# Four 16-row copies from SBUF to SBUF between the first loads of the GpSimd queue, in an eight-expert MoE kernel

## The chip, the core and the metric

The kernel runs on one core of a Trainium2 chip. The metric is the device time of one execution in microseconds (us); the median of 4 runs before the change is 183.47 us (183.39 to 183.78).

## The reference

Eight experts each apply a two-layer network to their own 256 rows of x. E = 8, T = 256, H = 512, M = 2048, all in float32:

```python
h = np.matmul(x, w1) + b1[:, np.newaxis, :]
h = np.maximum(h, 0)
return (np.matmul(h, w2) + b2[:, np.newaxis, :]).astype(np.float32)
```

x is (8, 256, 512), w1 is (8, 512, 2048), w2 is (8, 2048, 512); b1 and b2 are (8, 2048) and (8, 512). Each expert's w1 and w2 are 4 MB each in HBM, so the weights alone are 67 MB.

## The kernel before, in words

**Types and tiles.** The products run in fp16. DMAs issued by GpSimd convert on the way: they read float32 from HBM and write fp16 to SBUF. A w1 or w2 tile is 128 x 8192 fp16 (2 MB in SBUF, three buffers of each kind); an x tile is 128 x 1024 fp16 (256 KB, four buffers). The x of experts 0 and 1 comes as float32 by the SyncE and ScalarE queues (L188) and is cast by VectorE (L201). An output tile is 128 x 1024 float32, 512 KB, three buffers.

**Work per expert.** `first_product` (L108) multiplies the transposed x by w1 in 16 groups of four matmuls; ScalarE adds b1 and applies the ReLU to each (L120). Half-way, TensorE transposes the x of the next expert (L100). `second_product` (L151) starts from b2 by a one-row matmul (L163) and adds 32 matmuls of 512 columns (L175); VectorE and ScalarE each copy one half to the output tile (L138, L139). Step s of the last loop (L243) does the first product of expert s and the second of expert s - 3 (LAG = 3).

**What sets the order of the loads.** Nearly all transfers are DMAs issued by GpSimd, in one order written out by hand: the list `ring` (L221 to L241). Each entry has a step at which it may go, a function and its arguments; `ordered` keeps program order. The list begins at s = 1 with w1[1], and has for each later s the x of expert s (`load_x`, L69), the w1 of expert s (`load_w1`, L75), the w2 of expert s - 3 (`load_w2`, L85), and from s = 6 the store of the output of expert s - 6 (`flush`, L132). After it come eight pieces of the last expert's w2 (`load_w2_piece`, L91) with stores between them. w1[0] and the b2 row (L191, 8 KB) are issued ahead of the list. The last expert's output goes by SyncE and ScalarE (L142, L143, L149).

**What a DMA on GpSimd waits for.** A load waits until its buffer is free: a w1 tile for the first product of the expert three back, a w2 tile for the second product of the expert three back. Besides, the built program has eight completion semaphores for GpSimd's DMAs, given out in turn. A DMA that gets a semaphore again waits until the DMA that had it before, eight places ahead in GpSimd's order, has landed. GpSimd issues in order, so whatever stands behind a waiting DMA waits with it. In the text, w1[3] is the w1 of expert 3, out[0] the store of expert 0's output.

Of the kernel before, what the change touches and what calls it, by code (L numbers as in the profile page):

```python
# [11 lines left out]
def kernel(  # L12
# [9 lines left out]
    nc = tc.nc  # L22
    fp32 = mybir.dt.float32
# [3 lines left out]
    P = 128  # L27
# [4 lines left out]
    LAG = 3  # L32
# [5 lines left out]
    def ordered(ins):  # L38
        return tc.keep_in_program_order(ins)

    singles = ctx.enter_context(tc.tile_pool(name="singles", bufs=1))
# [14 lines left out]
    b2_sb = singles.tile([1, E * H], fp16)  # L56
    b1_rows = singles.tile([E * 2, M // 2], fp32)
    b1T = singles.tile([P, nJ, E], fp32)

    x16 = [None] * E  # L60
    xT = [None] * E
# [68 lines left out]
    def flush(e):  # L130
        dst, src = pending.pop(e)
        ordered(nc.gpsimd.dma_start(out=dst, in_=src))  # L132

    def store(e, po, c0, c1, split):
        w = c1 - c0
        pool = out_pool if w == H else singles
        out_sb = pool.tile([P, nTB, w], fp32, tag=f"out{c0}_{w}", name=f"out{w}")
        nc.vector.tensor_copy(out=out_sb[:, 0, :], in_=po[0])  # L138
        nc.scalar.copy(out=out_sb[:, 1, :], in_=po[1])  # L139
        dst = out[e].rearrange("(p tb) h -> p tb h", tb=nTB)[:, :, c0:c1]  # L140
        if split and c1 == H:
            nc.sync.dma_start(out=dst[:, 0, :], in_=out_sb[:, 0, :])  # L142
            nc.scalar.dma_start(out=dst[:, 1, :], in_=out_sb[:, 1, :])  # L143
        elif e in RING:
            pending[e] = (dst, out_sb)
        else:
            step = P // PARTS.get(e, 1)
            for lo in range(0, P, step):
                nc.sync.dma_start(out=dst[lo : lo + step], in_=out_sb[lo : lo + step])  # L149

    def second_product(e):  # L151
# [18 lines left out]
        for lo, hi, p0, p1, t in w2_sb[e]:  # L170
            mine = [b for b in blocks if p0 <= b[0] and b[1] <= p1]
            for tb in range(nTB):
                for j in range(lo, hi):
                    for c0, c1, _, _ in mine:
                        ordered(nc.tensor.matmul(  # L175
                            out=acc[c0, tb],
                            lhsT=hT[e][:, j, tb * P : (tb + 1) * P],
                            rhs=t[:, j - lo, c0 - p0 : c1 - p0],
                            start=False,
                            stop=(j == nJ - 1),  # L180
                        ))
            if hi == nJ:
                for c0, c1, _, _ in mine:
                    store(e, [acc[c0, tb] for tb in range(nTB)], c0, c1, e == E - 1)

    x32 = singles.tile([P, nXF32, nTB, H], fp32)
    for e in range(nXF32):
# [4 lines left out]
        out=b2_sb,  # L192
        in_=b2.rearrange("e h -> (e h)").rearrange("(o f) -> o f", o=1),
    ))
    make_identity(nc, ident)
    make_identity(nc, ident16)
    nc.vector.memset(ones1, 1.0)
# [6 lines left out]
    for j in range(nJ):  # L204
        for s in range(2):
            ordered(nc.tensor.matmul(  # L206
                out=pb[s * 64 : (s + 1) * 64, j, :, :],
# [5 lines left out]
    for s in range(2):  # L213
        nc.vector.tensor_copy(  # L214
            out=b1T[s * 64 : (s + 1) * 64, :, :], in_=pb[s * 64 : (s + 1) * 64, :, :, s]
# [4 lines left out]

    ring = []  # L221
    for s in range(1, E + LAG - 1):
        if s < E:
            if s >= nXF32:
                ring.append((s - 2, load_x, (s,)))
            ring.append((s - 2, load_w1, (s,)))
        if s >= LAG:
            ring.append((s - 2, load_w2, (s - LAG,)))
        if s >= 2 * LAG:
            ring.append((s - 2, flush, (s - 2 * LAG,)))  # L230
# [51 lines left out]
```

## Time and profile before

| | |
|---|---|
| median of 4 runs | 183.47 us (183.39 to 183.78) |
| the profiled execution: its time, its span | 183.44 us, 181.7 us |
| TensorE matmul, busy share of the span | 138.4 us, 76% |
| ScalarE / VectorE / GpSimd | 62.9 / 13.4 / 22.1 us |
| the GpSimd DMA queue, packets and share of 16 engines | 5872, 97.9% |
| GpSimd idle, until TensorE is done with a w1 buffer (L75) | 60.5 us, 5 times |
| GpSimd idle, until TensorE is done with a w2 buffer (L85) | 49.9 us, 4 times |

The span goes from the first to the last instruction that the profiler recorded; the execution's own time is 1.74 us longer. Busy times of one engine may lie beside those of the others. A row of slices cuts the span in 40 parts of 4.5 us, with the busy share of each in tenths. A DMA has two times: that of its issue by an engine, and that of its landing, when its completion semaphore has its full count; between them it stands in a queue of the 16 DMA engines.

### The profile page before, as it was taken

How to read it: one execution, taken by the hardware profiler on the slowest of the kernel's cores; microseconds unless marked ns; L12 is line 12 of the kernel's file. 1: busy time of each engine (PE TensorE's matmuls, PEld its weight loads, DVE VectorE, ACT ScalarE, POOL GpSimd, SP SyncE). 2: the span in 40 equal slices, each digit the busy share in tenths (PEclk: the TensorE clock that was granted, in tenths of full speed). 3: DMA queues.
4: the chain of work that ended last, by engine and by line, in shares of the span. 5: the costliest groups of instructions: out<-in, count | busy, mean ns of one | idle time of the engine just before them, and what ended most of it. 6: DMA issues, size and time to landing. Idle time of an engine off the chain costs nothing.

```text
span 181.7 us, 2204 instructions
## 1 busy us (share of the span) xinstructions
PE 138.4 (76%) x946; PEld 98.6 (54%) x946; DVE 13.4 (7%) x22; ACT 62.9 (35%) x138; POOL 22.1 (12%) x46
## 2 busy tenths in 40 slices
PE   0545979489550999849992999809999997999790
PEld 0544979469540854846481755708549743434560
DVE  0320101001000101010100101001010010101010
ACT  0022779539560330925063430903408701010000
POOL 7100030300300010211010000200004003113300
PEclk9999999969997599997999699995899999999998
DMA  5989998999899999999999999999899999999995
GB/s 187 286 177 233 231 220 184 211 251 220 186 231 231 209 195 231 198 239 198 231 231 198 206 231 227 177 285 216 191 231 216 281 195 276 211 239 287 216 280 192
DMA packets 7017, 40.58 MB, mean 223 GB/s; under 512 B 1216, under 2 KB 2256, under 8 KB 4960
## 3 DMA queue, kind: packets, MB, share of 16 engines
q0 software_dynamic: 5872, 38.81, 97.9%
q1 hardware_dynamic: 688, 0.95, 1.5%
q10 hardware_dynamic: 448, 0.69, 1.0%
q8 instruction: 7, 0.11, 0.2%
q14 instruction: 2, 0.02, 0.0%
HBM read 71.39 MB, written 4.19 MB: 416 GB/s over the span
## 4 chain that ended last, share of the span: by engine, by line
DMA 82%; PE 13%; POOL 2%; issue 1%; ACT 0%; POOLq 0%
DMA w2sb<-in_w_dram 39%; DMA x<-in_x_dram 24%; DMA w1sb<-in_w_dram 13%; PE ph L113 7%; DMA w<-in_w_dram 6%; PE acc L175 5%; PE psx L100 1%; POOL w1sb L75 1%; PE acc L163 0%; POOL b_sb L191 0%; POOL ident masks.py:199 0%; POOL w2sb L85 0%; POOL ident masks.py:197 0%; ACT out L139 0%; POOLq L266 0%
## 5 line engine op out<-in xcount | busy, mean ns | idle before, releaser
L113 PE MATMUL ph<-xT,w1sb 128*128 128x256 f16 x512 | 69.7, 304 | 9.9 <-DMA w1sb<-in_w_dram 9.9
L120 ACT ACTIVATE hT<-ph,b1T 128x256 f16<-128x256 f32 x128 | 57.1, 473 | 44.7 <-PE ph L113 44.5
L113 PEld LDWEIGHTS <-w1sb 128*128 128x128 f16 x512 | 62.3, 149 | 16.5 <-DMA w1sb<-in_w_dram 10.8
L175 PE MATMUL acc<-w2sb,hT 128*128 128x512 f16 x224 | 49.6, 379 | 1.1 <-DMA w2sb<-in_w_dram 1.1
L175 PEld LDWEIGHTS <-hT 128*128 128x128 f16 x288 | 27.1, 98 | 32.1 <-issue 6.0
L139 ACT COPY out<-acc 128x512 f32<-128x512 f32 (+2 forms) x9 | 4.9, 540 | 59.1 <-PE acc L175 59.1
L100 PE MATMUL psx<-ident,x 128*128 128x128 f16 x64 | 6.2, 254 | 20.0 <-DMA x<-in_x_dram 19.3
L100 PEld LDWEIGHTS <-x 128*128 128x128 f16 x64 | 5.0, 124 | 21.0 <-DMA x<-in_x_dram 20.2
L75 POOL DMA_DIRECT2D w1sb<-in_w_dram x8 | 4.4, 553 | 61.3 <-PE ph L113 60.5
L106 DVE COPY xT<-psx 128x1024 f16<-128x1024 f16 x8 | 5.5, 691 | 81.3 <-PE psx L100 81.3
L138 DVE COPY out<-acc 128x512 f32<-128x512 f32 (+2 forms) x9 | 5.7, 633 | 74.0 <-PE acc L175 74.0
L85 POOL DMA_DIRECT2D w2sb<-in_w_dram x8 | 4.3, 536 | 49.9 <-PE acc L175 49.9
L175 PE MATMUL acc<-w,hT 128*128 128x320 f16 (+1 forms) x64 | 7.8, 272 | 1.3 <-DMA w<-in_w_dram 1.3
L206 PE MATMUL pb<-ident,b_rows 16*64 16x16 f32 x64 | 3.7, 265 | 6.6 <-DMA b_rows<-in_b_dram 6.6
L206 PEld LDWEIGHTS pb<-ident,b_rows 16*64 16x64 f32 x64 | 3.6, 198 | 6.5 <-issue 6.5
L132 POOL DMA_DIRECT2D out_dram<-out x7 | 3.8, 542 | 21.7 <-ACT out L139 13.1
L91 POOL DMA_DIRECT2D w<-in_w_dram x8 | 5.0, 627 | 11.4 <-DMA w2sb<-in_w_dram 8.5
L120 ACT ACT_TABLE_LOAD x1 | 1.3, 1283 | 11.0 <-DVE b1T L214 11.0
L163 PE MATMUL acc<-b_sb,ones 1*128 1x512 f16 (+2 forms) x18 | 4.8, 355 | 0.0
L69 POOL DMA_DIRECT2D x<-in_x_dram x6 | 3.3, 545 | 5.4 <-DMA w2sb<-in_w_dram 4.6
L163 PEld LDWEIGHTS <-ones 1*128 1x128 f16 x18 | 1.1, 93 | 2.2 <-issue 2.1
L201 DVE CAST x<-x 128x1024 f16<-128x1024 f32 x2 | 1.4, 696 | 4.3 <-DMA x<-in_x_dram 4.3
(9 smaller groups left out, 2.6 us busy)
## 6 DMA issues: line engine op xcount, KB each, us to landing
w1sb<-in_w_dram POOLq DMA_DIRECT2D x8, 2048.0 KB, 33.6
w2sb<-in_w_dram POOLq DMA_DIRECT2D x6, 2048.0 KB, 45.5
out_dram<-out POOLq DMA_DIRECT2D x7, 512.0 KB, 27.3
w2sb<-in_w_dram POOLq DMA_DIRECT2D x2, 1024.0 KB, 24.1
x<-in_x_dram POOLq DMA_DIRECT2D x6, 256.0 KB, 39.0
w<-in_w_dram POOLq DMA_DIRECT2D x2, 384.0 KB, 18.7
x<-in_x_dram ACTq DMA_DIRECT2D x1, 512.0 KB, 5.2
x<-in_x_dram SPq DMA_DIRECT2D x1, 512.0 KB, 4.5
```

Of the source, the lines that this page charges most:

```text
L75: ordered(nc.gpsimd.dma_start(out=w1_sb[e], in_=w1[e].rearrange("(p kc) m -> p kc m", kc=nKC)))
L85: ordered(nc.gpsimd.dma_start(out=t[:, lo : lo + step, :], in_=src[:, lo : lo + step, :]))
L91: ordered(nc.gpsimd.dma_start(out=t, in_=src[:, lo:hi, c0:c1]))
L100: ordered(nc.tensor.transpose(out=pt[:, kc, tb * P : (tb + 1) * P], in_=x16[e][:, tb, :].rearrange("p (q kc) -> p q kc", kc=nKC)[:, :, kc] ...
L106: nc.vector.tensor_copy(out=xT[e], in_=pt)
L113: ordered(nc.tensor.matmul(out=ph, lhsT=w1_sb[e][:, kc, :].rearrange("p (q j) -> p q j", j=nJ)[:, :, j], rhs=xT[e][:, kc, :], start=(kc == 0),
L120: nc.scalar.activation(out=hT[e][:, j, :], in_=ph, func=mybir.ActivationFunctionType.Relu, bias=b1T[:, j, e : e + 1], scale=1.0,)
L138: nc.vector.tensor_copy(out=out_sb[:, 0, :], in_=po[0])
L139: nc.scalar.copy(out=out_sb[:, 1, :], in_=po[1])
L163: ordered(nc.tensor.matmul(out=t, lhsT=ones1, rhs=b2_sb[0:1, e * H + c0 : e * H + c1], start=True, stop=False,))
L175: ordered(nc.tensor.matmul(out=acc[c0, tb], lhsT=hT[e][:, j, tb * P : (tb + 1) * P], rhs=t[:, j - lo, c0 - p0 : c1 - p0], start=False, sto ...
L206: ordered(nc.tensor.matmul(out=pb[s * 64 : (s + 1) * 64, j, :, :], lhsT=b1_rows.rearrange("r (q j) -> r q j", j=nJ)[:, :, j], rhs=ident[0 ...
```

## The change

Two tiles are added: `zeros` (16 x 128 float32), which VectorE sets to 0 once, and `scratch` (16 x 4 x 128 float32). A new function `touch(i)` issues on GpSimd a DMA of `zeros` to slot i of `scratch`: 16 rows of 512 bytes, 8 KB. The list gets one `touch` at the head of each step s = 2, 3, 4 and 5, so ahead of x[2], x[3], x[4] and x[5]. Nothing reads `scratch`. Each copy takes a completion semaphore in the turn like any other DMA of GpSimd.

```diff
@@ -56,6 +56,8 @@
     b2_sb = singles.tile([1, E * H], fp16)
     b1_rows = singles.tile([E * 2, M // 2], fp32)
     b1T = singles.tile([P, nJ, E], fp32)
+    zeros = singles.tile([16, P], fp32)
+    scratch = singles.tile([16, 2 * LAG - 2, P], fp32)
 
     x16 = [None] * E
     xT = [None] * E
@@ -130,6 +132,10 @@
     def flush(e):
         dst, src = pending.pop(e)
         ordered(nc.gpsimd.dma_start(out=dst, in_=src))
+
+    def touch(i):
+
+        ordered(nc.gpsimd.dma_start(out=scratch[:, i, :], in_=zeros))
 
     def store(e, po, c0, c1, split):
         w = c1 - c0
@@ -192,6 +198,7 @@
         out=b2_sb,
         in_=b2.rearrange("e h -> (e h)").rearrange("(o f) -> o f", o=1),
     ))
+    nc.vector.memset(zeros, 0.0)
     make_identity(nc, ident)
     make_identity(nc, ident16)
     nc.vector.memset(ones1, 1.0)
@@ -220,6 +227,8 @@
 
     ring = []
     for s in range(1, E + LAG - 1):
+        if s > 1 and s < 2 * LAG:
+            ring.append((s - 2, touch, (s - 2,)))
         if s < E:
             if s >= nXF32:
                 ring.append((s - 2, load_x, (s,)))
```

## Prediction

> **What bounds the kernel now.** I read the slices first, then the DMA queues, then the chain of what ended last. From the page:
>
> ```profile
> DMA  5989998999899999999999999999899999999995
> ...
> q0 software_dynamic: 5872, 38.81, 97.9%
> ...
> HBM read 71.39 MB, written 4.19 MB: 416 GB/s over the span
> ## 4 chain that ended last, share of the span: by engine, by line
> DMA 82%; PE 13%; POOL 2%; issue 1%; ACT 0%; POOLq 0%
> ```
>
> The 16 DMA engines are busy in every slice but the first and the last. Nearly all of it (97.9% of their span) is one queue, the one that GpSimd fills. TensorE is busy 76% of the span and waits for the loads. So the time is the start, plus the sum of what the GpSimd queue carries, plus a tail after the last piece of w2. What an edit does counts only if it changes that sum or lets the queue run dry.
>
> How the queue drains is seen by adding, for a DMA, its start in GpSimd's timeline and its time to landing. The times to landing, one DMA each, of w1[0], the b2 row, w2[0], x[4], w1[4], w2[1], x[5], w1[5], w2[2], x[6], w2[3] and out[0], in this order (columns: what, issuer, count, KB, us to landing):
>
> ```profile
> w1sb<-in_w_dram POOLq DMA_DIRECT2D x1, 2048.0 KB, 14.3
> b_sb<-in_b_dram POOLq DMA_DIRECT2D x1, 8.0 KB, 13.8
> w2sb<-in_w_dram POOLq DMA_DIRECT2D x1, 2048.0 KB, 31.8
> x<-in_x_dram POOLq DMA_DIRECT2D x1, 256.0 KB, 32.5
> w1sb<-in_w_dram POOLq DMA_DIRECT2D x1, 2048.0 KB, 34.5
> w2sb<-in_w_dram POOLq DMA_DIRECT2D x1, 2048.0 KB, 43.7
> x<-in_x_dram POOLq DMA_DIRECT2D x1, 256.0 KB, 44.4
> w1sb<-in_w_dram POOLq DMA_DIRECT2D x1, 2048.0 KB, 43.5
> w2sb<-in_w_dram POOLq DMA_DIRECT2D x1, 2048.0 KB, 52.1
> x<-in_x_dram POOLq DMA_DIRECT2D x1, 256.0 KB, 52.0
> w2sb<-in_w_dram POOLq DMA_DIRECT2D x1, 2048.0 KB, 47.3
> out_dram<-out POOLq DMA_DIRECT2D x1, 512.0 KB, 47.9
> ```
>
> Issued at 25.96, 26.48, 34.18 and 34.69, the loads w2[0], x[4], w1[4] and w2[1] land at 57.8, 59.0, 68.7 and 78.4: one after another, 9.7 us per 2 MB tile and 1.2 us per x, however long before they were issued. The queue is served in the order of issue and has 30 to 50 us of work standing in it.
>
> GpSimd's own timeline shows what it waits for when it issues (start, duration, instruction, and the idle time before it with what ended it):
>
> ```profile
> 34.18 0.53 POOL L75 DMA_DIRECT2D w1sb<-in_w_dram  x1 [7.14 <-PE ph L113]
> 34.69 0.55 POOL L85 DMA_DIRECT2D w2sb<-in_w_dram  x1
> 35.21 0.56 POOL L69 DMA_DIRECT2D x<-in_x_dram  x1
> 46.46 0.53 POOL L75 DMA_DIRECT2D w1sb<-in_w_dram  x1 [10.69 <-PE ph L113]
> 46.98 0.55 POOL L85 DMA_DIRECT2D w2sb<-in_w_dram  x1
> 48.32 0.53 POOL L69 DMA_DIRECT2D x<-in_x_dram  x1 [0.80 <-DMA w1sb<-in_w_dram]
> ```
>
> The last wait is of a special kind. x[6] goes into a buffer that is long free; it waits for the landing of w1[3], which is the eighth DMA ahead of it. The program has eight completion semaphores for GpSimd's DMAs, used in turn, and a DMA waits until the one eight places earlier has landed.
>
> **The change, part by part.** Nothing is removed. Added are two small tiles, one memset of 16x128 on VectorE and four DMAs of 8 KB on GpSimd: t0 before x[2], t1 before x[3], t2 before x[4], t3 before x[5].
>
> The memset is VectorE's first instruction, ahead of the ones; behind it the casts of x wait 4.3 us for their DMA anyway, and that wait covers it. t0 needs it, but t0 comes after w1[1], issued at 3.29, and by then it is long done. Cost nothing; uncovered, it would be an instruction of some tenths of a us, once.
>
> The four issues cost GpSimd about 0.54 us each, as x's rows do, 2.2 us in all. They lie in its waits: t0 and t1 delay x[2], w1[2] and x[3] to about 6.0 at the latest, while the queue is still at w1[0] until 15.6; t2 and t3 stand ahead of waits of 7.14 and 10.69 us for TensorE. Cost nothing; without that cover, 2.2.
>
> The semaphore turn moves. For a DMA that has a copy among the eight ahead of it, the one it waits for is a later one than before. Read off the built program, with landings as above and the 0.28 us that the chain shows between such a landing and the issue: w2[1] now waits for w1[2] (landed 37.1), so its issue goes from 34.7 to about 37.4; x[5] waits for x[3], from 35.2 to about 39.2; w1[5] for w1[3], from 46.5 to 48.4; w2[2] for w2[0], from 47.0 to 58.1; x[6] for t2, from 48.3 to 58.6; out[0] for w2[1], from 73.5 to 78.8; x[7] for t3, from 78.6 to 79.3. w1[6], w2[3] and w1[7] stay with TensorE's release at 65.4, 72.9 and 85.3. From w1[7] on each DMA has the same partner eight places ahead as before, through the tail with its eight pieces of w2.
>
> Are these delays hidden? Each need only be issued before the queue gets to it. w2[1] is reached when w1[4] has landed, 68.7, so 31 us are left; w1[5] after x[5], 35.2 + 44.4 = 79.6, 31 left; w2[2] after w1[5], 46.5 + 43.5 = 90.0, 32 left; out[0] after w2[3], 72.9 + 47.3 = 120.2, 41 left; x[5], x[6] and x[7] have 39 and more. What hides them is the standing queue, and no margin is under 31 us. Cost nothing; if the cover were gone, the largest is 11 us.
>
> What is left is the work of the copies in the full queue. No row of before has a copy from SBUF to SBUF. The nearest is the b2 row: also 8 KB, also 16 packets of 512 bytes, also between two large loads in this queue. The end of it on the DMA engines, in the packets of 80 ns from 15.20 on:
>
> ```profile
> q0 software_dynamic: 3, 0.00, 8.0%
> ```
>
> 8.0% of 16 engines for 80 ns is 102 ns in three packets: the 4-byte completion of w1[0] on the last engine to get there, its 512-byte packet, and that packet's completion. In the packet records these start at 15.203, 15.225 and 15.265, and the next 16 KB packet at 15.286. So the small DMA holds the engine from 15.225 to 15.286, 0.061 us. The other side: the b2 row lands at 1.92 + 13.8 = 15.72, w1[0] at 1.26 + 14.3 = 15.56, so landing to landing it is 0.16. From below, a copy could cost nothing, if it fills a pause between packets; it can't gain by itself, as it moves bytes that nobody reads. I take 0.061, because what counts behind it is when the engine takes its next packet, and the next load's first packet does not wait for the landing. The SBUF source may be quicker than HBM; that lies inside the bounds.
>
> Sum: 4 x 0.061 = 0.24 us, bounds 0 and 4 x 0.16 = 0.64. All loads behind t3 land 0.24 later, the last pieces too, and TensorE's last matmuls, the two last evictions and stores follow them. The profiled execution took 183.44 with a span of 181.7, 1.74 outside it, which the change does not touch: 183.44 + 0.24 = 183.68. The median of the runs, 183.47, gives 183.71. I forecast **183.7**.
>
> The Trainium skill speaks against this ("DMA: Bandwidth & Descriptors", section "Anatomy of one DMA"): it gives a GpSimd DMA a fixed cost of about 2.0 us besides its bytes, mostly the wait for the write's receipt. Paid four times in series that would be an estimate of 8.1 us and a time of 191.5. The b2 row, 0.16 from landing to landing, says that in a full queue the receipt is waited for beside the next load, so I don't use it.
>
> **Rivals.** *Slower, by concentration.* A landing needs all 16 engines. If the 16 rows of a copy were put on one engine, that engine would carry 16 packets of 0.059 us (the record's duration), 0.94 us, and everything behind it would land by that much later. On four different engines that is 0.94 once, 184.4; on the same engine each time, 3.8, 187.2. It decides from 6 or more extra packets on the slowest engine (6 x 0.06 = 0.37, which is 0.2%). For it: the copy has 16 rows where large loads have 128. Against it: the b2 row's 16 packets start within 14.855 to 15.225, as the engines come free from w1[0], one on each. On the same page, "Why a DMA increments its semaphore by 16" has a transfer whose rows divide by 16 spread over 16 engines; no row here shows it for such a copy.
>
> *Slower, by the landing.* If each copy costs its whole 0.16, the sum is 0.64 and the time 184.1. For it: the source is new. Against it: the packet records of the b2 row.
>
> *No effect.* The copies go into pauses: 183.4 to 183.5. The program has the four DMAs where the diff puts them, so that they are not made is out; that they don't show is possible, as 0.24 is 0.13%.
>
> *Faster.* The engines do lose time now and then: from x[6], landed 48.32 + 52.0 = 100.3, to x[7] at 122.7, there are 22.4 us for w1[6], w2[3], out[0] and x[7], which by the other rows take 2 x 9.7 + 1.3 + 1.2 = 21.9. If other issue times avoid that 0.5, the result is 183.44 - 0.5 + 0.24 = 183.2; if also a similar loss in w1[1]'s slot (10.4 from the b2 row's landing to 26.16, instead of 9.7), 182.5. For it: issues do move. Against it: everything was in the queue long before, and the moves leave its order alone.
>
> **Numbers.** 0.2% of 183.47 is 0.37, about what a measurement of this kernel can tell from no change. Chances: the forecast 0.60 (183.5 to 183.9); no effect 0.12; landing price 0.13; concentration 0.07; faster 0.08, of which 0.07 beyond 0.2%. The forecast's upper edge adds 0.03 to slower. So faster 0.07, same 0.70, slower 0.23. The range of 8 in 10 takes in the bounds 0 and 0.64 with 0.1 for the spread of runs: 183.3 to 184.2; it leaves out concentration and most of faster.
>
> **What would show it.** In the profile after: q0 with 5872 + 4 x 32 = 6000 packets (16 of data and 16 completions a copy); the DMA slices as full as now; w2[2] issued near 58 instead of 47, out[0] near 79 instead of 73.5; later loads landing some 0.06 us later behind each copy, and x[7] near 122.9. I am wrong if a slice in the middle of the DMA row falls, if landings behind a copy are late by 0.2 or more, or if the tail has a new wait.

## The result and the profile after

The changed kernel takes 183.74 us (median of 42 runs, 183.43 to 184.29); beside it the kernel before takes 183.50 (63 runs, 183.02 to 184.05). The ratio is 1.0014, 95% interval 1.0009 to 1.0018: slower by 0.17 to 0.33 us. The profiled execution took 184.2 us with a span of 182.4, so it lies near the upper end of its own runs; a single profile, with a spread of 1 us between runs, can't show 0.24 us by its length.

The page of the changed kernel, first the slices, then the queue and the chain:

```profile
DMA  5998999999999999999999989999999999999994
...
q0 software_dynamic: 6000, 38.84, 97.7%
...
DMA 69%; PE 19%; issue 9%; POOL 1%; ACT 0%; POOLq 0%
```

The queue has 128 packets more (4 x 32), and it is still full from the second slice to the last but one. GpSimd's timeline (start, duration, instruction, idle time before it with what ended it):

```profile
34.07 0.53 POOL L77 DMA_DIRECT2D w1sb<-in_w_dram  x1 [6.00 <-PE ph L115]
37.30 0.53 POOL L87 DMA_DIRECT2D w2sb<-in_w_dram  x1 [2.70 <-DMA w1sb<-in_w_dram]
37.82 0.50 POOL L138 DMA_DIRECT2D scratch<-zeros  x1
39.13 0.55 POOL L71 DMA_DIRECT2D x<-in_x_dram  x1 [0.81 <-DMA x<-in_x_dram]
48.53 0.53 POOL L77 DMA_DIRECT2D w1sb<-in_w_dram  x1 [8.84 <-DMA w1sb<-in_w_dram]
57.93 0.53 POOL L87 DMA_DIRECT2D w2sb<-in_w_dram  x1 [8.88 <-DMA w2sb<-in_w_dram]
...
79.14 0.54 POOL L134 DMA_DIRECT2D out_dram<-out  x1 [5.20 <-DMA w2sb<-in_w_dram]
79.67 0.53 POOL L71 DMA_DIRECT2D x<-in_x_dram  x1
```

The new waits are there, 8.84 and 8.88 us where the kernel before had 10.69 for TensorE and none. Yet w1[5] and w2[2], issued at 48.53 and 57.93, land within about 0.5 us of where they landed before (89.5 and 99.2 against 90.0 and 99.0). In the landings of the trace, a copy lands 0.17 us behind the load ahead of it, and the x behind the copy 1.09: 1.27 for both at x[2], where x alone took 1.24.

What the prediction did not follow is the end. GpSimd closes the kernel with a long instruction called a drain, which begins with its last issue and ends after its last DMA has landed. The trace lists the closing drains of an engine in one row (durations in ns, shortest/median/longest, then first and last start). GpSimd's, first in the kernel before, then in the changed one:

```profile
L277 POOLq DRAIN  x3: 51/98/9357, 171.5 to 181.4; - x3
```

```profile
L286 POOLq DRAIN  x3: 46/102/9572, 172.0 to 182.1; - x3
```

The longest one starts at 171.53 before and 172.03 after, so it ends at 180.88 and 181.61. GpSimd's last DMA, the store of expert 6, has landed by then. Its time to landing (issued at 171.55), before:

```profile
out_dram<-out POOLq DMA_DIRECT2D x1, 512.0 KB, 7.7
```

and after (issued at 172.06):

```profile
out_dram<-out POOLq DMA_DIRECT2D x1, 512.0 KB, 7.8
```

That is 179.28 and 179.84 in the trace. So the drain goes on for 1.60 us after the last landing before, and 1.77 after. In both kernels the common end of all engines waits for it: SyncE's own drain is done at 180.78 before and 181.35 after, and the span ends 0.8 us after GpSimd's. SyncE's drains, before and after:

```profile
L277 SPq DRAIN  x3: 7/7/7, 180.7 to 181.1; - x3
```

```profile
L286 SPq DRAIN  x3: 7/7/13, 181.3 to 181.9; - x3
```

### The profile page after: what moved, and what is told of

Read it like the earlier page. It is cut to its first block, busy times and chain, and to the rows that moved or that the text cites. A ratio compares the mean times of both kernels' runs of the same rounds, so it can differ in the third digit from the quotient of the medians.

```text
span 182.4 us, 2210 instructions
## 1 busy us (share of the span) xinstructions
PE 138.7 (76%) x946; PEld 98.7 (54%) x946; DVE 13.5 (7%) x23; ACT 62.7 (34%) x138; POOL 24.5 (13%) x50
## 4 chain that ended last, share of the span: by engine, by line
DMA 69%; PE 19%; issue 9%; POOL 1%; ACT 0%; POOLq 0%
DMA w2sb<-in_w_dram 39%; DMA x<-in_x_dram 23%; PE acc L181 13%; DMA w1sb<-in_w_dram 8%; PE ph L115 5%; PE acc L169 1%; POOL w2sb L87 0%; POOL w1sb L77 0%; PE psx L102 0%; ACT out L145 0%; POOLq L87 0%; POOLq L275 0%; POOLq L134 0%
## 5 line engine op out<-in xcount | busy, mean ns | idle before, releaser
L115 PE MATMUL ph<-xT,w1sb 128*128 128x256 f16 x512 | 68.5, 300 | 9.0 <-DMA w1sb<-in_w_dram 9.0
L115 PEld LDWEIGHTS <-w1sb 128*128 128x128 f16 x512 | 61.6, 149 | 15.2 <-DMA w1sb<-in_w_dram 10.0
L181 PE MATMUL acc<-w2sb,hT 128*128 128x512 f16 x224 | 51.2, 388 | 2.6 <-DMA w2sb<-in_w_dram 2.6
L181 PEld LDWEIGHTS <-hT 128*128 128x128 f16 x288 | 27.6, 99 | 33.1 <-issue 8.0
L181 PE MATMUL acc<-w,hT 128*128 128x320 f16 (+1 forms) x64 | 7.3, 272 | 0.0
L138 POOL DMA_DIRECT2D scratch<-zeros x4 | 2.2, 539 | 0.0
```

The costliest lines, as they stand in the source:

```text
L115: ordered(nc.tensor.matmul(out=ph, lhsT=w1_sb[e][:, kc, :].rearrange("p (q j) -> p q j", j=nJ)[:, :, j], rhs=xT[e][:, kc, :], start=(kc == 0),
L181: ordered(nc.tensor.matmul(out=acc[c0, tb], lhsT=hT[e][:, j, tb * P : (tb + 1) * P], rhs=t[:, j - lo, c0 - p0 : c1 - p0], start=False, sto ...
```

## The experiments

All ratios are to the kernel before on the same chip, with 95% intervals; a difference in us is the ratio's distance from 1, times 183.5.

**Without the copies.** The call of `touch` is left out, tiles and memset stay.

```diff
-        if s > 1 and s < 2 * LAG:
-            ring.append((s - 2, touch, (s - 2,)))
```

> The two tiles and the memset of the change, without the four copies. Engine-work theory (a copy costs what it holds the DMA engines, about 0.03 us net in the packet records of the changed kernel, 0.11 us for four): no difference to before, within 0.1 us. Placement theory (the moved SBUF addresses or the memset cost something): +0.1 to +0.24 us. Issue-time theory (later issues of w1, w2, x and out cost the rest of the measured 0.24): no difference.

Measured: 1.0000 (0.9991 to 1.0009). Tiles, addresses and memset show no cost, to within 0.17 us.

**The waits without the copies.** GpSimd reads an element of a landed tile ahead of six DMAs:

```diff
+    def hold(i, tiles, e):
+        t = tiles[e]
+        t = t[0][4] if isinstance(t, list) else t
+        ordered(nc.gpsimd.tensor_copy(out=held[0:1, i : i + 1], in_=t[0:1, 0, 0:1]))
...
+            if s == 5:
+                ring.append((s - 2, hold, (3, w2_sb, 0)))
             ring.append((s - 2, load_w2, (s - LAG,)))
```

> No copies; six one-element copies by GpSimd itself, each of which reads a landed tile, put ahead of w2[1], x[5], w1[5], w2[2], x[6] and out[0], so that GpSimd issues these about when it does in the changed kernel (w2[2] near 58 us instead of 47, out[0] near 79 instead of 73.5). The DMA queue carries the same as before. Engine-work theory: no difference to before, within 0.1 us, as every margin is over 30 us. Issue-time theory: +0.13 to +0.24 us.

> The kernel with GpSimd's waits but no copies once more, as its first interval (0.9996 to 1.0013) has both no difference and the 0.13 to 0.24 us in it. Price theory: no difference, the two together within 0.1 us of before. Constant-of-the-issues theory: again +0.1 or more, and the two together clear of zero.

Measured: 1.0005 (0.9996 to 1.0013) and 1.0002 (0.9993 to 1.0011). The profile (of the first) has w2[2] and out[0] issued as in the changed kernel:

```profile
57.84 0.53 POOL L87 DMA_DIRECT2D w2sb<-in_w_dram  x1
...
79.08 0.54 POOL L134 DMA_DIRECT2D out_dram<-out  x1 [0.40 <-issue]
```
Together about +0.06 us, not clear of zero, and not clear of 0.1 either; this needed a stronger dose (below).

**Two copies at each place.** `touch` is called twice per step, with eight slots in `scratch`.

```diff
-            ring.append((s - 2, touch, (s - 2,)))
+            for k in range(2):
+                ring.append((s - 2, touch, (2 * (s - 2) + k,)))
```

> Two copies at each of the four places, eight in all. By the semaphore turn x[4] is then issued near 37 us and x[5] near 58 us, with 20 us of queue still standing. Engine-work theory: twice the copies, 0.22 us at 0.027 a copy, 0.49 at the 0.061 that the prediction took from the b2 row; about 183.7 to 184.0. Landing theory (0.17 us a copy): +1.4 us, 184.9. Issue-time theory: more than twice the change's cost, as issues move further.

Measured: 1.0024 (1.0016 to 1.0033), +0.44 us or 0.055 a copy. The landing theory is out. The price is nearer to 0.06 than to the 0.027 that the packet records show.

**Copies of 128 rows.**

```diff
-    zeros = singles.tile([16, P], fp32)
-    scratch = singles.tile([16, 2 * LAG - 2, P], fp32)
+    zeros = singles.tile([P, P], fp32)
+    scratch = singles.tile([P, 2 * LAG - 2, P], fp32)
```

> Four copies as in the change, but of 128 rows of 512 bytes each, so 8 packets an engine and copy instead of 1; order and semaphore turn are those of the change. Engine-work theory: 0.027 for the first packet with its completion and 7 x 0.037 us more (start to next start), 0.29 us a copy, 1.1 us in all: about 184.6. Fixed-cost-per-DMA theory and issue-time theory: as the change, +0.24, 183.7.

Measured: 1.0046 (1.0034 to 1.0058), +0.84 us. Bytes do cost, but my price for them was too high: the eight rows of an engine went as one packet of 4096 bytes, which holds an engine 0.16 us in the records, 0.64 for four copies. Again 0.2 us more was measured than the records give; 0.16 of it is what the table below gives for four more DMAs of GpSimd.

**Twenty copies, one ahead of each DMA.** The call of `touch` in the loop is gone, `scratch` is 128 x 3 x 128 so that each copy has its own 16 rows of a slot, and:

```diff
+    k = 0
+    while k < 20:
+        ring.insert(2 * k + 1, (ring[2 * k + 1][0], touch, (k,)))
+        k += 1
     e = E - LAG - 1
```

> Twenty copies of the change's size, one ahead of each of the twenty DMAs of GpSimd from x[2] to w2[5], so that there are never two in a row and four loads or stores of the old kind stay among any eight. The queue keeps 10 us or more standing throughout. Record theory (0.027 us net a copy, as the packets of the changed kernel show, and a constant of 0.1 to 0.2 that comes with later issues): 0.54 plus 0.1 to 0.2, 184.1 to 184.25. Price theory (0.06 us a copy and no constant, as the b2 row's packets and the times with 4 and 8 copies have it): +1.2 us, 184.7. Landing theory (0.17): +3.4, 186.9.

> Twenty copies of 512-byte rows once more, beside the two above on the same chip. Price theory (0.05 us a copy): +1.05 us, 184.5, as the first time (1.0044 to 1.0071).

Measured: 1.0057 (1.0044 to 1.0071) and 1.0058 (1.0046 to 1.0070), +1.05 and +1.06 us, 0.053 a copy. The record theory as I had put it is out. The drains of the first profile:

```profile
L288 POOLq DRAIN  x3: 46/103/10188, 171.6 to 182.3; - x3
```

The long one ends at 181.75, 2.42 us after GpSimd's last landing at 179.33.

**Its waits without the copies.** `hold`, as above, ahead of the DMAs from w2[0] to w2[5]:

```diff
+    tiles = {load_x: x16, load_w1: w1_sb, load_w2: w2_sb}
+    loads = list(ring)
+    for k in range(19, 3, -1):
+        _, put, args = loads[k - 3]
+        if put in tiles:
+            ring.insert(k + 1, (loads[k + 1][0], hold, (k, tiles[put], args[0])))
```

> No copies; GpSimd reads one element of a landed tile ahead of each load from w2[0] to w2[5], always of the load four places ahead, so that the loads are issued about when they are with twenty copies between them (at most three loads standing behind the one that lands). Price theory (0.05 us for each copy of GpSimd, nothing for later issues): no difference to before, within 0.15 us. Constant-of-the-issues theory (0.027 us a copy, the rest of what four, eight and twenty copies cost comes from later issues): +0.4 to +0.5 us, 184.0.

Measured: 0.9995 (0.9986 to 1.0003). Two rows of its timeline show how late the issues are:

```profile
90.55 0.53 POOL L87 DMA_DIRECT2D w2sb<-in_w_dram  x1 [0.31 <-POOL held L139]
...
99.80 0.54 POOL L134 DMA_DIRECT2D out_dram<-out  x1 [0.37 <-issue]
```

w2[3] is issued at 90.55 instead of 72.9 and out[0] at 99.80 instead of 73.5, and nothing is lost: the interval ends at +0.06 us. Later issues cost nothing measurable as long as the queue stands; that settles what the first two runs left open.

**Twenty copies of 4-byte rows.**

```diff
-        ordered(nc.gpsimd.dma_start(out=scratch[16 * (i % 8) : 16 * (i % 8) + 16, i // 8, :], in_=zeros))
+        ordered(nc.gpsimd.dma_start(out=scratch[16 * (i % 8) : 16 * (i % 8) + 16, i // 8, 0:1], in_=zeros[:, 0:1]))
```

> The twenty copies, each of 16 rows of 4 bytes instead of 512. Completion theory (most of a copy's price is the second DMA's completion and the change of DMAs, little of it data): +0.7 to +1.05 us, as much as or somewhat under the +1.05 of twenty copies of 512 bytes: 184.2 to 184.5. Data theory (the price is the 512-byte packet, 27 to 40 ns in the records): +0.2 to +0.4, 183.7 to 183.9.

Measured: 1.0041 (1.0029 to 1.0053), +0.75 us, 0.038 a copy. Most of the price comes with the DMA, not with its bytes.

**Thirty-two copies by SyncE.**

```diff
+    def copies(e):
+        for k in range(8):
+            ordered(nc.sync.dma_start(
+                out=scratch[16 * k : 16 * k + 16, e - 1, :], in_=w1_sb[e][0:16, 0, 0:256]
+            ))
...
             ring.append((s - 2, load_w1, (s,)))
+            if s < 5:
+                ring.append((s - 2, copies, (s,)))
```

> No copies by GpSimd; 32 copies of 16 rows of 512 bytes issued by SyncE instead, eight behind each of the landings of w1[1] to w1[4], out of the w1 tile. GpSimd's order, semaphore turn and issue times are those of before. Record theory (0.027 us net a copy): +0.9 us, 184.4. Price theory (0.06): +1.9, 185.4. If a copy costs only through the GpSimd queue and its semaphores: no difference, 183.5.

Measured: 1.0046 (1.0032 to 1.0059), +0.84 us, 0.026 a copy: half of what a GpSimd copy costs, and what the packet records give. That points to GpSimd for the other half. The drain's line of this kernel:

```profile
L287 POOLq DRAIN  x3: 51/99/9384, 172.4 to 182.4; - x3
```

It ends at 181.83, 1.60 us after GpSimd's last landing at 180.24, as in the kernel before.

**Eight copies at each place.**

```diff
-            ring.append((s - 2, touch, (s - 2,)))
+            for k in range(8):
+                ring.append((s - 2, touch, (8 * (s - 2) + k,)))
```

> Eight copies at each of the four places. Now the last copy of each group takes the semaphore of the load just ahead of the group, so GpSimd stops until that load has landed, and the queue runs dry behind w1[1], w1[2], w2[0] and w2[1]. Semaphore-turn theory: each time about 0.28 us from landing to issue, 0.54 for the copy, 0.55 for x and about 2 us (an estimate from the last stores, 3.0 us from issue to landing) before data flows again, so about 3 us a place, 12 in all, and 32 x 0.03 to 0.06 of work on top: 196 to 198. Work-only theory (the turn never matters): +0.9 to +1.9, 184.4 to 185.4.

Measured: 1.1011 (1.0987 to 1.1036), 201.8 us. The turn of the semaphores does matter once its cover is gone, and more than I expected. The busy times in the four stretches behind w1[1], w1[2], w2[0] and w2[1] (columns: engines, then the granted clock, the share of the DMA engines, GB/s):

```profile
26.00:31.00 5.00, 4.65 (x45) 4.42 (x46) 0.00 (x0) 3.97 (x9) 4.68 (x10) 1.00 0.62 110
...
41.00:46.00 5.00, 4.86 (x23) 3.80 (x24) 0.00 (x0) 2.23 (x5) 4.56 (x10) 0.50 0.60 107
...
65.00:70.00 5.00, 0.50 (x5) 0.50 (x6) 0.00 (x0) 0.00 (x0) 4.57 (x10) 0.50 0.55 107
...
90.00:95.00 5.00, 0.17 (x2) 0.18 (x3) 0.00 (x0) 0.00 (x0) 4.43 (x9) 0.58 0.64 107
```

The DMA share falls to about 0.6 in each, where the changed kernel has 0.98 to 1.03 in the same stretches. GpSimd's timeline of the first one shows the stop:

```profile
26.32 0.49 POOL L138 DMA_DIRECT2D scratch<-zeros  x1 [9.58 <-DMA w1sb<-in_w_dram]
26.79 0.57 POOL L71 DMA_DIRECT2D x<-in_x_dram  x1
27.35 0.56 POOL L77 DMA_DIRECT2D w1sb<-in_w_dram  x1
```

The eighth copy waits for w1[1], landed at 26.04; x[2] is issued at 26.79 and lands at 30.46, 4.4 us after w1[1] instead of 1.24. The four places lose 3.2, 3.4, 3.1 and 3.4 us this way, 13 in all, and behind three of them the first 2 MB load takes 0.9 longer than usual. By w2[3] the landings are 17.2 us late. And the end is longer too:

```profile
L287 POOLq DRAIN  x3: 46/103/10697, 188.5 to 199.8; - x3
```

From 188.55 to 199.24; the last landing is at 196.33. The drain takes 2.91 us after it.

**The drain, measured in every profile.** The profiles side by side show where GpSimd's part lies. "Drain" is from the landing of GpSimd's last DMA to the end of its long drain; "end" from the landing of the last store to the end of the span.

| kernel | GpSimd DMAs | drain, us | end, us |
|---|---|---|---|
| before | 38 | 1.60 | 1.03 |
| waits alone (three profiles), tiles alone | 38 | 1.60 | 1.02 to 1.07 |
| 32 copies by SyncE | 38 | 1.60 | 1.04 |
| the change | 42 | 1.77 | 1.19 |
| four copies of 128 rows | 42 | 1.76 | 1.19 |
| two at each place | 46 | 1.93 | 1.37 |
| twenty (both profiles) | 58 | 2.42 | 1.86, 1.87 |
| twenty of 4-byte rows | 58 | 2.42 | 1.85 |
| eight at each place | 70 | 2.91 | 2.34 |

In every profile the drain is 0.04 us plus 0.041 us for each DMA that GpSimd has issued in the whole kernel, whatever it carried. The last run asks whether that is what reaches the time.

**Twenty copies with the drain covered.** GpSimd's last two DMAs are left out, so the drain can work while the last stores are still on their way.

```diff
     for e in LATE:
-        ring.append((e + LAG + 1, flush, (e,)))
+        ring.append((e + LAG + 1, pending.pop, (e,)))
```

> The twenty copies of 512-byte rows, with GpSimd's last two DMAs, the stores of experts 5 and 6, left out, so that two eighths of the output are not written. Drain theory (at its end GpSimd works off about 0.041 us for each DMA that it has issued, after the last of them has landed: 1.60 us in the profile with 38 DMAs, 2.42 with 58, 2.91 with 70): with 56 DMAs the drain takes 2.34 us, but starts from the landing of the last piece of w2 near 176.8 and ends near 179.1, before SyncE's and ScalarE's last stores land. So the copies' 0.82 us at the end are covered, the span ends 1.03 us after the last store lands as without copies (instead of 1.87), and the time is 183.0 to 183.8. Queue-price theory (0.05 us for each copy in the queue, the end not special): the last piece still lands some 1 us later than without copies, or the span still ends 1.87 us after the last store, and the time stays near 184.3 to 184.6.

Measured: 0.9992 (0.9983 to 1.0002), 183.42 us. Its profile:

```profile
L288 POOLq DRAIN  x3: 46/98/11003, 168.9 to 181.9; - x3
```

From 168.91 to 179.92. The last piece of w2 lands at 177.57, so the drain takes 2.35 us after it, as 56 DMAs should (2.34), and it is done before SyncE's last store lands at 181.24. The span ends 0.91 us after that. The copies' part of the drain is off the path. The queue-price theory is out: twenty copies no longer cost 1 us.

There is no control without copies and without the two stores, but the traces bound what the missing stores give back. They stand behind the last piece of w2 in the queue, so what they can hold up is the last stores of SyncE and ScalarE. SyncE's last one takes 2.76 us from issue to landing here and 3.02 to 3.06 in the kernels before and after and with twenty copies: 0.28 us, not 1. The drain no longer sticks out behind it, which gives 0.12 more than before had (0.91 instead of 1.03). Of these 0.40 us the run shows 0.15 (by its interval from 0.31 to none). The rest, some 0.25 us or 0.012 a copy, is an estimate of the copies' work in the queue; the two lengths in it come from single profiles.

## Why the prediction was right, point by point

**The time** was forecast at 183.7, without a measurable difference by its bound of 0.37 us; it is 183.74, +0.24 us. The interval, 0.17 to 0.33, has the 0.24 of the forecast in its middle. The sum was right, but not its terms.

**"0.061 a copy" of work in the full queue** is the term that was mis-sized. The b2 row reads HBM, its packets take 59 ns; a copy's take 40, and on an engine a copy delays the next packet by 0.027 us in the records. Thirty-two copies by SyncE cost 0.026 each. For GpSimd's copies, what is left of the times beside the drain is 0.012 us each with twenty copies (1.05 - 0.82 = 0.23, over 20; both intervals reach from about zero to 0.024), and -0.07 us for all twenty of 4 bytes. So the change has between nothing and 0.11 us of it, some 0.05 by the twenty copies, not 0.24. Why twenty copies cost less in the queue than their packets show (20 x 0.027 beside the drain's 0.82 would be 1.36, above both intervals) stays open.

**"All loads land 0.24 later, the last evictions and stores follow"** failed by what it left out. The prediction followed the path to the last store and took the rest of the span as fixed. It isn't: GpSimd's drain ends last, and each DMA lengthens it by 0.041, four by 0.16. The drain ended only 0.10 us after SyncE's in the kernel before, so little would have been seen of it had SyncE's stores come 0.2 us later. 0.16 for the drain and up to 0.11 for the queue make 0.16 to 0.27, and 0.17 to 0.33 was measured. That 0.041 for the drain and 0.01 to 0.027 for the queue come near the 0.061 of the b2 row is chance: the forecast had the right sum from one term that was too large and one that was missing. The prediction named a new wait in the tail as a sign of being wrong; the wait for the drain was there before, but is 0.17 us longer.

**The moved issues** came where the prediction had them: w2[1] at 37.30 (forecast 37.4), x[5] 39.13 (39.2), w1[5] 48.53 (48.4), w2[2] 57.93 (58.1), x[6] 58.45 (58.6), out[0] 79.14 (78.8), x[7] 79.67 (79.3). That they cost nothing measurable is shown by the waits without copies, most sharply by the one that moves out[0] to 99.80. That the cover is what makes them free is shown by eight copies at each place, +18 us.

**The memset** costs nothing measurable, as forecast (1.0000 without the copies). **The four issues** no run shows by themselves; the 2.2 us by which they hold GpSimd up are less than the delays that cost nothing in the waits without copies.

**The rivals.** Landing price: a copy does land 0.17 us behind its predecessor, but the DMA behind it goes on meanwhile; 4, 8 and 20 copies exclude 0.16 each. Concentration: the 16 packets of each copy start on the engines as each gets done with the load ahead, within 1.2 to 1.4 us of each other, and the x behind the first copy lands 1.09 after it; had one engine carried 16 of them, 0.64 us at 0.040 each, twenty copies would have shown it. Faster: nothing of it. The lost 0.5 us around w2[3] did not go away: in the changed kernel's profile that slot is 10.8 us instead of 10.2, and in the others with a standing queue 9.7 to 10.6. This varies from execution to execution; its cause was not settled, and it is most of the 0.7 us by which this one span is longer than the other.

**"x[7] near 122.9"** was not met in the profile, 123.4, for the same slot.

**The Trainium skill's 2.0 us** a DMA ("DMA: Bandwidth & Descriptors", "Anatomy of one DMA") would have made 8.1 us; rightly not used here, since the queue was full. Where the queue was empty, in the run with eight copies, x[2] took 3.7 us from issue to landing, 2.4 more than the 1.24 that an x takes in the full queue, so a cost of that kind is paid there.

## What to carry to other kernels

In a queue that stands full, when a DMA is issued does not matter and a tiny extra one took hundredths of a us here; ask how much work still stands in the queue at the issue, and only where that runs out (here with eight copies in a row) price the wait. Follow the path past the last store to the end of the span: which engine's last instruction ends last, and what makes it long. Where GpSimd's DMAs are among the last, as here, every DMA it issued counts there (0.041 us each), so a second price for each is to be added, or GpSimd is to be done earlier than the other queues.

## What the runs showed of the hardware that I had not expected

**The drain.** GpSimd's closing drain ends 0.04 + 0.041 n us after the landing of its last DMA, n being all DMAs it issued (1.60 at 38 to 2.91 at 70), independent of their size. SyncE's drains in the same profiles take 7 to 13 ns. The Trainium skill ("VectorE: DVE Perf Modes", section "The DRAIN you can't avoid") describes the closing drains as about 12 ns on all engines; that agrees with SyncE's and not with GpSimd's, and here the measurement decides.

**Small DMAs beside large ones.** SyncE's copies landed some 2.46 us apart while 16 KB packets were in the GpSimd queue (52.68, 55.14, 57.60), though SyncE had issued them 0.63 us apart; median 9.1 us from issue to landing. That is as long as two 16 KB packets, 1.21 us each; read so, a copy's data waits for one and its completion for another. It agrees with the same skill's "DMA: Bandwidth & Descriptors", section "Queues, rings and completion order": an engine changes between queues at packets only.
